# A DeltaNet layer in a streaming encoder: low parts of its weights on GpSimd, the state update in four row strips, the end of an inverse in whole-array products

## The chip, the cores and the metric

The kernel runs on one core of one Trainium2 chip. The metric is the device time of one execution in microseconds (us), lower is better. Engines are named as the profile names them: PE is TensorE (PEld its weight loads), DVE is VectorE, ACT is ScalarE, POOL is GpSimd and SP is SyncE, which issues most transfers.

## The reference

One inference step of a two-layer encoder for 384 tokens: 8 running streams of 16 tokens and one new stream of 256. Layer 0 mixes tokens by a convolution module, layer 1 by a gated DeltaNet; each layer has two SwiGLU sublayers and a cross-attention beside that. All is float32. The change concerns the DeltaNet of layer 1 (8 heads of 128):

```python
def gated_deltanet(h, conv_buf, S0, w_in, conv_w, a_log, dt_bias, norm_g, w_out):
    proj = h @ w_in
    ...
    qkv = jax.nn.silu(causal_depthwise_conv(hist, conv_w)).astype(F32)
    q, k, v = jnp.split(qkv, 3, axis=-1)
    q = l2_normalize(q.reshape(B, L, DN_HEADS, DN_HEAD_DIM)) * (DN_HEAD_DIM ** -0.5)
    ...
    o, S = chunk_gated_delta_rule(q, k, v, g, beta, S0.astype(F32))
    o = rms_norm(o, norm_g) * jax.nn.silu(gate.astype(F32).reshape(B, L, DN_HEADS, DN_HEAD_DIM))
    y = o.reshape(B, L, DN_WIDTH).astype(h.dtype) @ w_out
```

Within a block of tokens the rule solves a unit lower triangular system, and the state is carried on from block to block:

```python
    a_mat = jnp.where(strict, kk, 0.0) + jnp.eye(C, dtype=F32)
    sol = lax.linalg.triangular_solve(a_mat, rhs, left_side=True, lower=True, unit_diagonal=True)
    ...
        u = vc_i - jnp.einsum('bhck,bhkv->bhcv', kc_i, S)
        o = jnp.einsum('bhck,bhkv->bhcv', q_i, S) + jnp.einsum('bhij,bhjv->bhiv', qk_i, u)
        S = S * ge_i + jnp.einsum('bhck,bhcv->bhkv', kd_i, u)
```

## The kernel before, in words

**Tiles.** The 384 tokens are three tiles of 128: tile 0 the eight running streams (16 tokens each, so a strip of 32 partitions holds two streams), tiles 1 and 2 the new stream. Weights come in chunks of 128 x 1024 words.

**Weights in two parts.** TensorE multiplies a rounded type fast, so `get` (L276) loads a chunk, has ScalarE round it (high part, `whi`), and has VectorE subtract to get what the rounding lost (low part, `wlo`, L287, the operation itself in the helper `tt`, L197 in the profile). A projection (`proj` L725 with `gmm` L658) is then 24 products of 384 columns: for each of 8 slices of the depth high x high, high x low and low x high. Three raw and eight split chunks are on chip (L30, L31).

**Order of the work.** The program is recorded first. A main stream records projections one by one; generators (tasks) record what hangs on them, such as a head. `Scheduler.order` (L383) then sorts all recorded operations by a list schedule: each operation has a cost from a table in the helpers, the one with the longest way to the end goes first, and each engine gets a fixed order from it. Buffers and PSUM banks were given out while recording (eight banks, `_bank` L545, `gbank` L565), so a dependence through a bank is a dependence of the schedule too.

**The DeltaNet sublayer** (`deltanet`, L1249). The main stream projects gates first, then q, k, v of each head and the output gates z: 33 chunks (L1594 to L1610), then 8 chunks of the output projection (L1609). `short` (L1350) is the short convolution of one projected tile, with history copies on GpSimd (L215). `head` (L1369) does one head beside the main stream; a head's core waits for that of the head two before it (L1373), a q projection for the core of three before (L1598).

**The inverse** (`unit`, L1421), one for each of the three token tiles: blocks of up to 32 tokens are inverted by doubling, with masks that VectorE multiplies in (`apart`, L1433, two operands in SBUF) and products of 64 or 32 columns on TensorE. For tiles 1 and 2 the blocks of 32 are joined to 64 and these to 128; the last two products (L1464, L1467) use a quarter of the array:

```python
e = E.mm(g[64:128, 0:64], a[0:64, 64:128], x[0:64, 0:64], True, True)
e = E.act(y[64:128, 0:64], g[64:128, 0:64], dep=e, scale=-1.0)
yield max(e, e2)
e = E.mm(g[0:64, P:P + 64], y[64:128, 0:64], u[64:128, 64:128], True, True)
```

**The state's part of the running streams** is read by four products at once on tiles of 128 rows by 32 columns (`quad` L250, used at L1492).

**The state update** of the eight streams (L1541 to L1552), at the end of a head's core: in two rounds ScalarE makes four copies of `u`, each with the tokens of all but one stream set to zero (`K_BM`), TensorE multiplies the keys of all 128 tokens with the four copies (128 x 128 by 512 columns, float32, which TensorE does in two passes), and VectorE adds the 512 columns to the state. The state is then stored (L270).

Of the kernel before, what the change touches and what calls it, by code (L numbers as in the profile page):

```python
# [8 lines left out]
F32 = mybir.dt.float32  # L9
# [6 lines left out]
P = 128  # L16
D = 1024
KT = 8                  # feature tiles of d_model
NTOK = 384              # columns: 128 of the sample group (8 streams x 16), then 256 of the prompt
TT = 3                  # token tiles: sample, prompt 0, prompt 1  # L20
FF = 22                 # feature tiles of d_ff
NB = 8                  # sample streams
BL = 16                 # tokens of one
NH = 8                  # DeltaNet heads
XH = 4                  # cross-attention heads
# [4 lines left out]
W = 8                   # split weight chunks on chip  # L30
RAW = 3                 # raw chunks on chip  # L31
# order of the first transfers: memory (m), key and value chunks (c), rows (x), identity, gains
START = ["c0a", "m0a", "c0b", "m0b", "m1", "i", "x1", "g", "c1", "x2", "x0", "c2"]
TOLD = CW - BL          # taps that reach no token of the same step
OLD = 10                 # feature tile of the first sublayer from which these are worked on
CHB = 4000.0            # ns by which what belongs to a token tile goes before the same of the next
RUSH = 10000.0          # ns by which a sublayer's last projections go before the rest
NRUSH = 3               # feature tiles that this holds for
SLOTS = 4               # chunks of keys and values on chip at the start
FOUR = ["f01", "f10", "f11", "x0", "x1"]     # sublayers whose first 512 features are made token tile by token tile  # L40
# first projections of a sublayer that begin before the last token tile is there
SPLIT = {"f00": 0, "conv": 0, "x0": 1, "f01": 0, "f10": 0, "dn": 1, "x1": 2, "f11": 0}
# pieces of the memory's keys and values that a place in the program offers the tensor engine
KV = {"start": 3, "f00": 3, "conv": 20, "co": 3, "xo": 0, "f01": 1, "f10": 2, "dn": 6, "f11": 0}
HALF = 1400.0            # ns by which the first half of a row goes before the second
GROUPS = [(0, 1), (2, 3, 4, 5, 6, 7)]   # heads whose decays are made together
TAIL = 3                # down-projection chunks that go token tile by token tile
LANES = 8               # transfers under way on a queue
DMA_IN, DMA_OUT = 650.0, 950.0
HOP = 100.0             # ns from an engine to the next  # L50
BIG = 17300             # words of the shared region

# columns of the per-feature table
# [5 lines left out]
# constant matrices: causal blocks, block sums, decay masks, block-doubling masks  # L59
# [34 lines left out]
class Emitter:  # L94
    """Records the program in issue order. Tasks beside the main stream are advanced by running
    clocks of the engines, so that their matmuls fall where their operands are ready."""
# [153 lines left out]
    def quad(self, mms):  # L250
        """Products into four groups of 32 rows, which the tensor engine works on at once."""
        n = self._n(mms[0][2])
        cost = 2 * max(107.0, n / 1.2) + 85.0
        self.vt += cost
        t = self.nc.tensor

        def go():
            for out, lhsT, rhs, start, stop in mms:
                t.matmul(out, lhsT, rhs, start=start, stop=stop)  # L259
        self._add("P", cost, go, [x for m in mms for x in m[1:3]], [m[0] for m in mms])  # L260
        return self.vt + HOP

# [13 lines left out]
    def get(self, name, dest=None):  # L276
        """The two parts of a weight chunk: loaded and split as early as their room is free."""
        j = self.nchunk
        self.nchunk += 1
        raw = self.raw[j % RAW]  # L280
        hi, lo = dest if dest is not None else (self.hi[j % W], self.lo[j % W])
        assert dest is not None or j - W < 0 or self.held[j % W] is None, "a chunk is still in use"
        if dest is None:
            self.held[j % W] = j
        self.load(raw, self.wall[CHUNK[name]])
        self.act(hi, raw)
        self.tt(lo, raw, hi.bitcast(F32), ALU.subtract)  # L287
        return j, hi, lo
# [15 lines left out]
class Scheduler:  # L304
    """Orders the recorded program: a list schedule by the longest way to the end, on the engines'
    known costs, that keeps every dependence between the operations."""
# [8 lines left out]
    def cell(self, ap):  # L315
        """(what, bits): the tile and the columns in it that an operand covers."""
# [32 lines left out]
    def graph(self):  # L349
        ops = self.ops  # L350
        readers, writers = {}, {}
        for i, o in enumerate(ops):
# [3 lines left out]
            for what, bits in rs:  # L356
                if what is not None:
                    pred.update(j for b, j in writers.get(what, ()) if b & bits)
                    if what[0:2] == "ps":
                        # two engines don't read a bank at once  # L360
# [79 lines left out]
class Region:  # L440
    """First-fit allocation of the columns of one tile."""
# [5 lines left out]
    def take(self, n, keep=0, high=False):  # L447
# [13 lines left out]
        # of the places at an edge of a hole, the one whose columns were freed the longest ago  # L461
# [19 lines left out]
class Model:  # L481
# [42 lines left out]
    def alloc(self, n, keep=0):  # L524
        """(columns, handle) for the main stream."""
# [19 lines left out]
    def _bank(self):  # L545
# [3 lines left out]
        # the one that has been free for longest  # L549
# [38 lines left out]
    def rows(self, kind, i):  # L588
        """A row of gains on all partitions."""
# [4 lines left out]
    def rstd(self, s1, s2, dep):  # L594
        """(s1 + s2) ** -0.5."""
# [6 lines left out]
    def chain(self, t, y, yb, gpost, gpre, half=False, cross=False):  # L602
        """x += post(y); the next sublayer's normalized input, transposed and split."""
# [8 lines left out]
        if y is not None:  # L612
            ss, s0 = self.st(2), self.st(1)
            f = 4.0 if half else 1.0    # half of the norm: a root of four times the mean square
            for n in range(2):
                # the two banks, one to an engine at a time
# [15 lines left out]
        for n in range(2):  # L632
# [3 lines left out]
            # behind the row stands what its sum of squares is short of  # L636
# [21 lines left out]
    def gmm(self, out, hi, lo, c0=0, c1=NTOK, h=None, l=None):  # L658
        """out[feature, token] of a chunk [k, 8, 128 features] and the transposed activations."""
# [12 lines left out]
    def dmm(self, y, hi, lo, ah, al, first, last, halves=(0, 1)):  # L672
        """y[token, 1024] += activations [k, 128 tokens] times a chunk of rows."""
# [9 lines left out]
    def first_chunks(self, names, chains, split):  # L683
        """The first projections of a sublayer; some of them on two token tiles before the third is there."""
# [18 lines left out]
    def wide(self, o, w, t):  # L703
        """out[token, 512] of a token tile and four pieces of weights [k, 2, 512]."""
# [14 lines left out]
    def turn(self, a, o, e):  # L719
        """Four blocks of columns, transposed."""  # L720
# [4 lines left out]
    def proj(self, name):  # L725
        j, hi, lo = self.E.get(name)
# [5 lines left out]
    def gains(self, post, pre):  # L732
        """Rows of gains: of the norm behind a sublayer and of the next one's."""
# [98 lines left out]
    def tokenwise(self, acc, held, ops, ready, first, gpost, gpre, ghs, before=None, kv=0, late=False, half=False):  # L832
        """The last chunks of a product into the residual, token tile by token tile, each followed by
        its norms in the background."""
# [30 lines left out]
    def kv_open(self, slots=2, order=()):  # L865
        """Room for pieces of the memory's keys and values: the memory, some weight chunks, two results."""
# [14 lines left out]
    def early(self, what, order):  # L881
        """The first transfers of all go in a given order."""
        self.E.bonus = 1e9 - 1e6 * order.index(what) if what in order else 0.0

    def kv_part(self, out, name, what, order):
        """One of the first transfers in two halves, so that the products can begin with the first."""
# [16 lines left out]
    def kv(self, n):  # L903
        """Some pieces of the memory's keys and values. They wait for nothing else and go where the
        tensor engine would stand still."""
# [40 lines left out]
    def old_taps(self):  # L946
        """The taps that reach only tokens of earlier steps for all of a step's tokens."""
# [17 lines left out]
    def conv(self, chains, post, pre):  # L965
# [4 lines left out]
        HW = CW - TOLD + BL - 1     # tokens of a block and those before it that the later taps reach  # L970
# [27 lines left out]
        def taps():  # L998
            for c0 in range(0, KT, 2):
# [5 lines left out]
                for j in range(CW):  # L1005
                    for c in cs:
# [4 lines left out]
                        elif j < TOLD:  # L1011
                            # the prompt's tokens that have a token that far behind
# [236 lines left out]
    def deltanet(self, chains, post, pre):  # L1249
# [40 lines left out]
        def pre_task(o, b, e):  # L1290
            """Gates of all heads and the decays between all tokens."""
# [39 lines left out]
            for hs in GROUPS:  # L1331
# [12 lines left out]
                # one behind the other, so that the scalar engine changes its table once  # L1344
# [5 lines left out]
        def short(o, b, e, ti):  # L1350
            """Short convolution and SiLU of one feature tile; (columns, handle, ready)."""
# [17 lines left out]
        def head(h, q, k, v):  # L1369
# [51 lines left out]
            def unit(t):  # L1421
                """Decayed products of keys and queries, and the inverse's transpose by block doubling."""
# [6 lines left out]
                # blocks of up to 32 tokens lie one below the other in 32 columns: the transposes of the  # L1429
                # inverse so far and of what it makes of the matrix, which one product brings on together  # L1430
# [21 lines left out]
                if t:  # L1452
                    # pairs of blocks of 32 tokens, then the two of 64
# [10 lines left out]
                    e = E.mm(g[64:128, 0:64], a[0:64, 64:128], x[0:64, 0:64], True, True)  # L1464
                    e = E.act(y[64:128, 0:64], g[64:128, 0:64], dep=e, scale=-1.0)
                    yield max(e, e2)
                    e = E.mm(g[0:64, P:P + 64], y[64:128, 0:64], u[64:128, 64:128], True, True)  # L1467
# [21 lines left out]
            # sample: the state's part of the keys and queries, even and odd streams apart  # L1489
# [4 lines left out]
            # prompt, first chunk: no state yet  # L1494
# [46 lines left out]
            (UM, umh) = yield from room(512)  # L1541
# [248 lines left out]
```

## Time and profile before

| what | value |
|---|---|
| median of three runs | 1893.7 us (1892.61 to 1894.55) |
| span of the profiled execution | 1891.9 us |
| VectorE, ScalarE, GpSimd busy in it | 1025.5, 794.5, 168.8 us |
| mean granted TensorE clock | 0.998 |
| HBM | 146 GB/s over the span |

The profiled execution is one more run beside the three timed ones; its own time is known by its span, and 1.8 us lie between the span and the median of the runs. Rows of the profile give line, engine, operation, output<-inputs and shape, then the count, busy time, and the mean of one in ns. In a listing by time the first two numbers are start and length in us. TensorE's instructions are pipelined: their lengths overlap, and what one costs is read from the starts. A float32 product stands as two records, one for each pass.

### The profile page before, as it was taken

What the parts mean: (1) busy time and instruction counts of PE and PEld (TensorE: products, weight loads), DVE (VectorE), ACT (ScalarE), POOL (GpSimd) and SP (SyncE); (2) the same over time, 40 slices, a digit from 0 to 9 for tenths busy, and PEclk for the clock granted to TensorE, in tenths of its full rate; (3) what the DMA queues carried; (4) which work ended last, traced back from release to release, by engine and by line L of the source; (5) the groups of instructions that cost most, each with busy time, mean ns of one, the idle gap of its engine ahead of it and who ended that gap; (6) DMA issues with size and microseconds to landing.
All of it is one profiled execution on the core that took longest, in us unless ns stands there. A gap on an engine that the chain in (4) does not pass through costs nothing.

```text
span 1891.9 us, 27912 instructions
## 1 busy us (share of the span) xinstructions
PE 1870.6 (99%) x10863; PEld 1682.6 (89%) x10863; DVE 1025.5 (54%) x1940; ACT 794.5 (42%) x1589; POOL 168.8 (9%) x407
## 2 busy tenths in 40 slices
PE   8999999999999999999999999999999999999998
PEld 7999999999877899999899999989898767899997
DVE  6564436998653633334633344788886734533333
ACT  4333334312643533233433233787786533433332
POOL 1000002111100100000100000323321101000000
PEclk9999999999999999999999999999999999999999
DMA  8544434556685443434533343433324782444431
GB/s 300 179 136 125 134 112 121 128 147 216 219 312 210 156 129 128 134 123 130 163 122 117 120 134 101 128 97 99 123 90 124 236 311 101 134 134 134 122 123 45
DMA packets 88469, 278.83 MB, mean 147 GB/s; under 512 B 18001, under 2 KB 20561, under 8 KB 88337
## 3 DMA queue, kind: packets, MB, share of 16 engines
q1 hardware_dynamic: 86080, 271.42, 44.7%
q0 software_dynamic: 2256, 5.64, 0.9%
q8 instruction: 85, 1.39, 0.3%
q14 instruction: 48, 0.39, 0.1%
HBM read 265.09 MB, written 11.92 MB: 146 GB/s over the span
## 4 chain that ended last, share of the span: by engine, by line
PE 97%; ACT 1%; DMA 1%; DVE 0%; POOL 0%; issue 0%; SPq 0%; DVEq 0%; POOLq 0%; ACTq 0%
PE ps L247 91%; PE ps L266 3%; PE ps L259 2%; DMA raw<-in_w 0%; POOL stat L197 0%; ACT big L190 0%; DMA x<-in_x 0%; DVE big L210 0%; ACT whi L189 0%; SPq L270 0%; ACT big L189 0%; ACT hTl L190 0%; ACT L190 0%; DVE big L197 0%; DVE wlo L197 0%
## 5 line engine op out<-in xcount | busy, mean ns | idle before, releaser
L197 DVE TENSOR_TENSOR wlo<-raw,whi 128x1024 fp32r<-128x1024 f32 x361 | 438.1, 1221 | 570.7 <-ACT whi L189 542.7
L189 ACT CAST whi<-raw 128x1024 fp32r<-128x1024 f32 x361 | 374.5, 1050 | 640.3 <-PE ps L247 584.6
L247 PE MATMUL ps<-hTh,wlo 128*128 128x384 f32 x1680 | 498.3, 341 | 0.0
L247 PE MATMUL ps<-hTl,whi 128*128 128x384 f32 x1680 | 497.1, 342 | 0.0
L247 PE MATMUL ps<-hTh,whi 128*128 128x384 f32 (+1 forms) x1680 | 496.9, 342 | 0.0
L247 PEld LDWEIGHTS ps<-hTl,whi 128*128 128x128 f32 x1680 | 308.9, 188 | 8.0 <-issue 2.1
L247 PEld LDWEIGHTS ps<-hTh,whi 128*128 128x128 f32 x1680 | 308.8, 188 | 7.9 <-issue 1.2
L247 PE MATMUL ps<-big 128*128 128x128 f32 (+5 forms) x1944 | 308.0, 288 | 7.1 <-DMA big<-in_w 6.7
L247 PEld LDWEIGHTS ps<-hTh,wlo 128*128 128x128 f32 x1680 | 308.7, 188 | 6.5 <-issue 2.3
L247 PEld LDWEIGHTS ps<-big 128*128 128x128 f32 (+1 forms) x1944 | 269.6, 190 | 40.3 <-issue 20.8
L247 PE MATMUL ps<-whi,rbh 128*128 128x512 f32 x672 | 206.0, 396 | 0.4 <-ACT big L189 0.4
L247 PE MATMUL ps<-wlo,rbh 128*128 128x512 f32 x672 | 203.8, 395 | 0.0
L247 PE MATMUL ps<-whi,rbl 128*128 128x512 f32 x672 | 202.5, 393 | 0.0
L210 DVE SCALAR_TENSOR_TENSOR big<-big,cols 128x384 f32<-128x384 f32 (+13 forms) x424 | 189.5, 497 | 2.2 <-ACT big L190 0.3
L247 PEld LDWEIGHTS ps<-whi,rbl 128*128 128x128 f32 x672 | 125.7, 188 | 24.7 <-issue 0.4
L247 PEld LDWEIGHTS ps<-wlo,rbh 128*128 128x128 f32 x672 | 125.3, 188 | 24.6 <-issue 0.4
L247 PEld LDWEIGHTS ps<-whi,rbh 128*128 128x128 f32 x672 | 124.8, 188 | 21.1 <-ACT big L189 0.6
L197 DVE TENSOR_TENSOR big<-big,ps 128x64 f32<-128x64 f32 (+4 forms) x219 | 86.4, 405 | 39.8 <-PE ps L247 39.2
L266 PE MATMUL ps<-ident,big 128*128 128x128 f32 x479 | 89.5, 279 | 5.5 <-DVE big L210 5.4
L247 PE MATMUL ps<-whi,hTh 128*128 128x512 f32 x240 | 87.2, 399 | 0.7 <-ACT hTh L189 0.7
L189 ACT COPY big<-ps 32x32 f32<-32x32 f32 (+5 forms) x155 | 49.6, 324 | 90.2 <-PE ps L247 64.3
L247 PE MATMUL ps<-whi,hTl 128*128 128x512 f32 x240 | 86.3, 398 | 0.0
(82 smaller groups left out, 1350.7 us busy)
## 6 DMA issues: line engine op xcount, KB each, us to landing
raw<-in_w SPq DMA_DIRECT2D x362, 512.0 KB, 3.8
big<-in_w SPq DMA_DIRECT2D x37, 512.0 KB, 5.1
big<-in_ck SPq DMA_DIRECT2D x32, 512.0 KB, 6.5
big<-in_cv SPq DMA_DIRECT2D x32, 512.0 KB, 6.3
big<-in_npre SPq DMA_DIRECT2D x8, 512.0 KB, 7.5
out_pkv<-big POOLq DMA_DIRECT2D x32, 128.0 KB, 5.0
big<-in_npost SPq DMA_DIRECT2D x8, 512.0 KB, 7.3
big<-out_pkv SPq DMA_DIRECT2D x8, 512.0 KB, 5.1
```

The costliest lines, as they stand in the source:

```text
L189: return self._on("A", cost, dep, lambda: sc.copy(out, in_), [in_], w)
L197: return self._on(eng, cost, dep, lambda: e.tensor_tensor(out=out, in0=a, in1=b, op=op), [a, b], [out])
L210: lambda: v.scalar_tensor_tensor(out=out, in0=a, scalar=s, in1=b, op0=op0, op1=op1), [a, s, b], [out])
L247: self._add("P", cost, lambda: t.matmul(out, lhsT, rhs, start=start, stop=stop, **kw), [lhsT, rhs], [out])
L259: t.matmul(out, lhsT, rhs, start=start, stop=stop)
L266: self._add("P", 109.0, lambda: t.transpose(out, in_, ident), [in_, ident], [out])
```

## The change

Three edits, all inside the DeltaNet sublayer. Comments and docstrings were removed from the file as well.

1. `get` and `proj` take an engine. With "G" the low part is made by GpSimd, in two halves of 512 columns. The projections of the DeltaNet other than its first two chunks (31 chunks) and its 8 output chunks are made so; high parts stay on ScalarE, and all other sublayers stay as they were.
2. The last two products of the inverse take whole operands (128 rows, 128 columns of weights) and still 64 columns. The rows of the result that were not made before are not read, and the additional rows that are multiplied in hold zeros in the other operand.
3. The state update: ScalarE makes two masked copies of `u` (even streams, odd streams; `K_EO`), and four products follow, each on a strip of 32 tokens: its strip of the keys with 256 columns, into a bank of its own. VectorE adds four times 256 columns.

```diff
+    def strips(self, mms):
+        n = self._n(mms[0][2])
+        cost = 2 * max(107.0, n / 1.2) + 170.0
+        self.vt += cost
+        t = self.nc.tensor
+        def go():
+            for out, lhsT, rhs in mms:
+                t.matmul(out, lhsT, rhs, start=True, stop=True)
+        self._add("P", cost, go, [x for m in mms for x in m[1:3]], [m[0] for m in mms])
+        return self.vt + HOP
...
-    def get(self, name, dest=None):
+    def get(self, name, dest=None, eng="V"):
...
-        self.tt(lo, raw, hi.bitcast(F32), ALU.subtract)
+        if eng == "V":
+            self.tt(lo, raw, hi.bitcast(F32), ALU.subtract)
+        else:
+            for c in (slice(0, 512), slice(512, 1024)):
+                self.tt(lo[:, c], raw[:, c], hi[:, c].bitcast(F32), ALU.subtract, eng=eng)
...
-    def proj(self, name):
-        j, hi, lo = self.E.get(name)
+    def proj(self, name, eng="V"):
+        j, hi, lo = self.E.get(name, eng=eng)
...
-                    e = E.mm(g[64:128, 0:64], a[0:64, 64:128], x[0:64, 0:64], True, True)
+                    e = E.mm(g[:, 0:64], a, x[:, 0:64], True, True)
                     e = E.act(y[64:128, 0:64], g[64:128, 0:64], dep=e, scale=-1.0)
                     yield max(e, e2)
-                    e = E.mm(g[0:64, P:P + 64], y[64:128, 0:64], u[64:128, 64:128], True, True)
+                    e = E.mm(g[:, P:P + 64], y, u[:, 64:128], True, True)
...
-            (UM, umh) = yield from room(512)
-            bbm_ = cst[:, K_BM:K_BM + 8]
-            o, b = yield from self.gbank()
-            for j in range(2):
-                for n in range(4):
-                    em = E.act(tc_(UM, n), tc_(u, 0), dep=e4, scale=bbm_[:, 4 * j + n:4 * j + n + 1])
-                yield em
-                e4 = E.mm(o, tc_(kd, 0), UM, True, True)
-                c = slice(512 * j, 512 * j + 512)
-                e5 = E.tt(S[:, c], S[:, c], o, ALU.add, dep=max(e4, es2))
-                yield e5 - 800
+            (UM, umh) = yield from room(256)
+            for n in range(2):
+                em = E.act(tc_(UM, n), tc_(u, 0), dep=e4, scale=cst[:, K_EO + n:K_EO + n + 1])
+            (o0, b0), (o1, b1) = (yield from self.gbank()), (yield from self.gbank())
+            (o2, b2), (o3, b3) = (yield from self.gbank()), (yield from self.gbank())
+            yield em
+            os_ = (o0, o1, o2, o3)
+            r4 = [slice(32 * j, 32 * j + 32) for j in range(4)]
+            e4 = E.strips([(os_[j][:, 0:256], kd[r4[j], 0:P], UM[r4[j], :]) for j in range(4)])
+            for j in range(4):
+                c = slice(256 * j, 256 * j + 256)
+                e5 = E.tt(S[:, c], S[:, c], os_[j][:, 0:256], ALU.add, dep=max(e4, es2))
             E.load(self.O["sstate"][h], S)
-            self.bfree(b)
+            self.bfree(b0, b1, b2, b3)
...
-            o, b, e = fc[1] if n == 0 else self.proj((kind, h))
+            o, b, e = fc[1] if n == 0 else self.proj((kind, h), "G")
...
-        held = [E.get(("do", h)) for h in range(NH)]
+        held = [E.get(("do", h), eng="G") for h in range(NH)]
```

The costs in the helpers serve the ordering alone. For GpSimd the helper `tt` (L192) books 130 + 2.3 n ns for n columns, for VectorE 65 + 1.05 n; the new `strips` books 170 ns over the streaming of 256 columns in two passes, where `quad` books 85.

## The prediction

> **What bounds the kernel now.** The profile page first: span, engines, and the chain that ended last.
>
> ```profile
> span 1891.9 us, 27912 instructions
> PE 1870.6 (99%) x10863; PEld 1682.6 (89%) x10863; DVE 1025.5 (54%) x1940; ACT 794.5 (42%) x1589; POOL 168.8 (9%) x407
> PE 97%; ACT 1%; DMA 1%; DVE 0%; POOL 0%; issue 0%; SPq 0%; DVEq 0%; POOLq 0%; ACTq 0%
> ```
>
> TensorE (PE) is busy all the time and is 97% of the chain: what ends later or earlier is decided by the length of TensorE's own list, unless another engine makes it stand still. The profiled span, 1891.9 us, is 1.8 us under the median of the runs, 1893.7; I take that 1.8 as unchanged and subtract from the median.
>
> The change lies in the DeltaNet sublayer alone. Its products lie between about 1185 and 1485 us of the span, so the second view is the busy time by stage for that stretch (POOL is GpSimd), and for 30 us inside it in which VectorE (DVE) is fullest.
>
> ```profile
> core 0: us, PE busy (x) PEld busy (x) DVE busy (x) ACT busy (x) POOL busy (x), PEclk, DMA share, GB/s
> 1185.00:1485.00 300.00, 299.64 (x1997) 270.00 (x1995) 235.15 (x777) 225.20 (x667) 78.84 (x226) 1.00 0.35 113
> 1310.00:1340.00 30.00, 30.00 (x212) 26.28 (x211) 27.40 (x100) 23.41 (x79) 10.24 (x27) 1.00 0.36 113
> ```
>
> TensorE 299.64 of 300 at full clock; VectorE 235 (78%), ScalarE (ACT) 225 (75%), GpSimd 79 (26%). Even with VectorE at 27.4 of 30 (91%) TensorE did not stop. So here time off VectorE or ScalarE is worth nothing by itself, and time off TensorE's list is worth its full amount as long as the others follow.
>
> **What a product costs TensorE.** An instruction's own duration overlaps the next one's, so I read costs from starts, in the order of time. First a whole-array product of 64 columns among projections:
>
> ```profile
> 1417.18 0.33 PE L247 MATMUL ps<-hTl,whi 128*128 128x384 f32 x1
> 1417.35 0.33 PE L247 MATMUL ps<-hTh,wlo 128*128 128x384 f32 x1
> 1417.52 0.34 PE L247 MATMUL ps<-hTh,whi 128*128 128x384 f32 x1
> 1417.70 0.33 PE L247 MATMUL ps<-big 128*128 128x64 f32 x2
> 1417.84 0.42 PE L247 MATMUL ps<-hTl,whi 128*128 128x384 f32 x1
> 1418.10 0.34 PE L247 MATMUL ps<-hTh,wlo 128*128 128x384 f32 x1
> ```
>
> Projections follow each other every 0.175 us. From 1417.52 to 1418.10 are 0.58 us with two of them, so the float32 product between (two records) costs 0.58 - 0.35 = 0.23. Now the quarter-array product of the inverse:
>
> ```profile
> 1316.48 0.33 PE L247 MATMUL ps<-hTl,whi 128*128 128x384 f32 x1
> 1316.65 0.34 PE L247 MATMUL ps<-hTh,wlo 128*128 128x384 f32 x1
> 1316.92 0.74 PE L247 MATMUL ps<-big 64*64 64x64 f32 x4
> 1317.42 0.42 PE L247 MATMUL ps<-hTh,whi 128*128 128x384 f32 x1
> 1317.68 0.38 PE L247 MATMUL ps<-big 128*128 128x128 f32 x2
> ```
>
> The row of four holds the 64x64 product and a whole-array one behind it. 1316.65 to 1317.68 are 1.03; less two projections (0.35) and that whole-array product (0.23) the small one costs 0.45, twice the whole-array form: the projection ahead of it takes 0.27 instead of 0.175, and there is a toll behind it too. Third, the four products on 32-column tiles at once (L259), the form nearest to the new strips:
>
> ```profile
> 1250.55 0.44 PE L247 MATMUL ps<-hTh,wlo 128*128 128x384 f32 x1
> 1250.83 0.33 PE L247 MATMUL ps<-big 128*128 128x64 f32 x2
> 1250.96 0.42 PE L247 MATMUL ps<-hTh,whi 128*128 128x384 f32 x1
> 1251.32 0.64 PE L259 MATMUL ps<-big 128*32 128x256 f32 x8
> 1251.89 0.49 PE L247 MATMUL ps<-big 128*128 128x128 f32 x2
> 1252.13 0.42 PE L247 MATMUL ps<-hTl,whi 128*128 128x384 f32 x1
> 1252.39 0.27 PE L247 MATMUL ps<-big 128*128 128x128 f32 x1
> ```
>
> 1250.83 to 1252.39 are 1.56; less two projections and two whole-array products (0.81) the four cost 0.75 with both tolls. Fourth, the state update's product today:
>
> ```profile
> 1262.02 0.42 PE L247 MATMUL ps<-hTh,wlo 128*128 128x384 f32 x1
> 1262.27 0.34 PE L247 MATMUL ps<-hTh,whi 128*128 128x384 f32 x1
> 1262.45 1.02 PE L247 MATMUL ps<-big 128*128 128x512 f32 x2
> 1262.91 0.74 PE L247 MATMUL ps<-hTl,whi 128*128 128x384 f32 x1
> 1263.48 0.44 PE L247 MATMUL ps<-big 128*128 128x64 f32 x3
> ```
>
> 1262.27 to 1263.48 are 1.21; less two projections, 0.86 for one 128x512 float32 product.
>
> **The change part by part.** The counts first.
>
> ```profile
> L247 PE MATMUL ps<-big 128*128 128x512 f32 x32 | 16.4, 594 | 0.0
> L247 PE MATMUL ps<-big 64*64 64x64 f32 x64 | 10.2, 243 | 0.2 <-ACT big L189 0.2
> L197 DVE TENSOR_TENSOR wlo<-raw,whi 128x1024 fp32r<-128x1024 f32 x41 | 49.5, 1212 | 14.8 <-ACT whi L189 12.8 <-PE ps L247 2.0
> L210 DVE SCALAR_TENSOR_TENSOR big<-big,cols 128x384 f32<-128x384 f32 x72 | 43.4, 606 | 0.6 <-ACT big L190 0.3
> L197 DVE TENSOR_TENSOR big<-big 128x128 f32<-128x128 f32 x168 | 42.7, 277 | 0.5
> L197 DVE TENSOR_TENSOR big<-big,ps 128x512 f32<-128x512 f32 x14 | 9.4, 675 | 2.0 <-PE ps L247 2.0
> L190 ACT ACTIVATE big<-big 128x128 f32<-128x128 f32 x148 | 49.7, 383 | 8.8 <-DVE big L197 3.7 <-PE ps L247 2.9 <-PE ps L259 1.5
> ```
>
> *State update.* Two records make one float32 product, so the first row is 16 products, two to a head: 2 x 0.86 = 1.72 us a head go. Four strips of 32 tokens by 256 columns come. No trace shows strips of rows. If they overlap as the column tiles do they cost 0.75; if not at all, eight records of half a 512-column record (0.43, half of 0.86, so 0.215) are 1.72 plus the two tolls of about 0.1 each, 1.92. I take 0.86: the column tiles' price, and 0.1 because each strip loads weights of 128 columns, not 32, in both passes (the projection behind the shape change at 1250.55 takes 0.28 instead of 0.175, which is my measure of such a load with nothing to cover it). Saving 8 x 0.86 = 6.9 us, ends 7.8 and -1.6. The Trainium skill (TensorE: Matmul & The Clock Gate, Part 3, measured speedup against the span model) gives 3.07 times for four row strips of 512 columns; by it the eight records would take 0.56, with the tolls 0.76, and the saving would be 7.7.
>
> *Inverse.* 64 records are 32 products at 0.45, replaced one for one by whole-array products of 64 columns at 0.23: 0.22 each where one stands alone. Some stand beside another small-tile product and share a toll; I take 0.2, 6.4 us, ends 3.2 (every second toll shared) and 7.0.
>
> *ScalarE and VectorE in the state update.* Six of eight masked copies a head go: 48 x 0.383 = 18 us off ScalarE. VectorE's two adds of 512 columns become four of 256: between 277 ns (128) and 675 ns (512) lies 0.41, so 4 x 0.41 - 2 x 0.675 = 0.29 more a head, 2.3 us. From the masked copies to the last add a head's chain shortens from 2 x (4 x 0.383 + 0.86) + 0.675 = 5.5 us to 2 x 0.383 + 0.86 + 4 x 0.41 = 3.3. None of it is on TensorE's path today.
>
> *Low parts.* 31 projection and 8 output chunks: 39 x 1.212 = 47 us leave VectorE, 78 halves of 512 columns come to GpSimd. GpSimd's price for them is in no row; its nearest are copies:
>
> ```profile
> 1227.12 0.18 POOL L215 COPY big<-big 128x3 f32<-128x3 f32 x1
> 1233.20 0.21 POOL L215 COPY big<-big 128x32 f32<-128x32 f32 x1 [0.97 <-DVE big L210]
> 1289.54 1.14 POOL L215 COPY big<-big 128x24 f32<-128x24 f32 x1 [0.78 <-DVE big L210]
> 1289.39 1.22 DVE L197 TENSOR_TENSOR wlo<-raw,whi 128x1024 fp32r<-128x1024 f32 x1
> ```
>
> 0.03 us for 29 more columns is 1 ns a column: 0.7 us for 512 with one input, about 1.2 if the second input is read as slowly. I take 1.2, 94 us in all; ends 0.7 (55 us) and 2 (156 us). GpSimd would then be busy 173 of some 287 us. TensorE needs a low part only 24 products (4.2 us) at the soonest behind the previous chunk's, eight chunks have buffers, so two halves of 1.2 and a wait stay hidden; without that cover each would cost 2.4 - 1.2 = 1.2 us, 47 in all. Queued behind a half on GpSimd: the history copies that the short convolutions wait for, the some 15 small operations from which a head takes its scales, the sums and powers of the norms at both ends of the stage, and stores of keys and values. Each can come up to 1.2 us later.
>
> *The two engines in each other's way.* The last two rows: a copy that takes 0.21 took 1.14, from 1289.54 to 1290.68, 0.07 behind the end of the 1.22 us subtraction on VectorE that had begun before it. So a GpSimd read waits for a VectorE operation with two operands in SBUF. The Trainium skill (SBUF — State Buffer, SBUF: two separate sides) calls the shared port pair an exclusive lock for a whole instruction, in both directions; the trace agrees in this direction, 1.14 us against 0.21, and the other is not seen, as GpSimd's operations are short today. I price the other direction from rows: two SBUF operands have the 72 and the 168 of the list, 240 operations. With 94 us of halves in 287 a third of them meet one, with 0.6 us left: 240 x 0.33 x 0.6 = 47 us (ends 0 and 100). That is just what leaves: VectorE would stand at 235 - 47 + 2 + 47 = 237 of 287 us, 83%, below the 91% at which TensorE still ran. What I charge is latency: of a head's 21 two-operand steps in the inverse, some 8 in a row meet it, 8 x 0.2 = 1.6 us, with some 2 for GpSimd's queue, less the 2.2 by which the state update's chain shortens: 1.5 us at the last head, where no later projections cover it.
>
> *Whole operands, banks.* The whole-array forms read columns that were written earlier anyway: nothing. A state update holds four of eight PSUM banks for the strips and their adds instead of one: nothing as long as projections find a bank; otherwise see below.
>
> Sum: -6.9 - 6.4 + 1.5 = -11.8, 1881.9, say 1882.
>
> **The rivals.** *Banks (and the planner's new order).* With four banks held, TensorE's next projection waits for one. Each such wait is at most the four adds, 1.6 us; half of that for each of eight heads, and 6.4 us come back: 1888. For it: a head's unit holds its bank through the whole inverse. Against: today's wait for a bank isn't visible, PE 299.64 of 300.
>
> *Strips run one behind another.* Then the part that promises most does not do what it says: +1.6 in place of -6.9, 1890.4. Against: the L259 rows begin all eight records in 0.57 us.
>
> *VectorE becomes the bound (slower).* If a two-operand operation waits longer than I think, VectorE passes 91% of 287 us, 261. That needs 71 us of waits, 0.30 us for each of the 240, where I have 0.2. At 0.4 us, 96: 286 us of work, a stage of 286 / 0.91 = 314 instead of 300, and 1908. For it: every GpSimd copy caught behind a 1.2 us operation waited it out, and 78 such operations would now stand on the other side. Against: halves are spread, and a waiting VectorE operation gets in between two.
>
> **How the numbers follow.** Forecast 0.64 (1876 to 1886: strips 0.75 to 1.0, inverse 3.2 to 7.0, up to 3 us of waits), banks 0.18, strips in a row 0.07, VectorE 0.11. The range reaches from 1876 to 1893, which leaves out the VectorE case. 0.2%, 3.8 us, is about what a measurement of this kernel can tell from no change; faster means under 1889.9: 0.64, 0.14 of the banks' case and 0.03 of the strips in a row make 0.81; 0.08 lie within; 0.11 slower.
>
> **What would show it.** Right: eight strip groups whose records start within 0.05 us of each other, twice, and no 64x64 rows; the stage 11 to 13 us shorter; PE still over 99% in it; VectorE's rows for two SBUF operands longer or with idle time while a half runs; GpSimd's halves near 1.2 us. Wrong: strip records 0.2 us apart; TensorE idle with VectorE or GpSimd as releaser in the stage; halves over 2 us.

## The result, and the profile after

The change made the kernel slower: 1942.5 us (median of four runs, 1938.46 to 1943.55) against 1893.9 (four runs, the profiled one with them), a ratio of 1.0257 with a 95% interval of 1.0244 to 1.0269, 48.6 us. The page of the changed kernel, the lines that answer to those of before:

```profile
span 1936.7 us, 27984 instructions
PE 1886.9 (97%) x10895; PEld 1695.8 (88%) x10895; DVE 1036.5 (54%) x1917; ACT 781.2 (40%) x1539; POOL 261.6 (14%) x485
PE 88%; DVE 7%; ACT 2%; DMA 1%; issue 1%; POOL 1%; SPq 0%; DVEq 0%; POOLq 0%; ACTq 0%
```

TensorE's share of the chain fell from 97% to 88%, and VectorE, which had none, has 7%. The busy time by stage, for the DeltaNet (now some 350 us instead of 300), and for 14 us inside it:

```profile
core 0: us, PE busy (x) PEld busy (x) DVE busy (x) ACT busy (x) POOL busy (x), PEclk, DMA share, GB/s
1185.00:1535.00 350.00, 320.54 (x2055) 286.93 (x2054) 249.68 (x763) 213.84 (x625) 170.46 (x308) 0.95 0.32 105
1343.00:1357.00 14.00, 10.17 (x48) 7.60 (x48) 12.94 (x47) 4.09 (x18) 6.38 (x15) 0.53 0.36 117
```

TensorE is busy 320 of 350 us where it was busy 299.6 of 300, and its granted clock is 0.95, in the short stretch 0.53. VectorE has lost 47 us of subtractions and is still busy 250 us, but that is only 71% of the stage. Its groups in this stage, and GpSimd's halves (that last row is of the whole execution; 74 of the 78 lie in these 350 us):

```profile
L197 DVE TENSOR_TENSOR big<-big 128x128 f32<-128x128 f32 x168 | 64.7, 400 | 1.0
L210 DVE SCALAR_TENSOR_TENSOR big<-big,cols 128x384 f32<-128x384 f32 x72 | 60.4, 842 | 0.8
L215 DVE COPY big<-big 128x45 f32<-128x45 f32 x24 | 10.2, 426 | 7.5 <-ACT big L189 7.3
L197 DVE TENSOR_TENSOR big<-big,ps 128x256 f32<-128x256 f32 x32 | 12.3, 402 | 1.4 <-PE ps L272 1.4
L197 POOL TENSOR_TENSOR wlo<-raw,whi 128x512 fp32r<-128x512 f32 x78 | 104.3, 1347 | 313.0 <-ACT whi L189 312.3
```

The masks of the inverse take 400 ns instead of 277, the taps of the short convolution 842 instead of 606: those are the operations with two operands in SBUF. These are means: counted one by one, 42 of the 240 take over 0.1 us longer than usual, 0.87 us on average, and the others take what they took before. The adds that read PSUM are at 402, as interpolated (410). A listing by time shows one case from start to end:

```profile
1340.21 2.81 POOL L197 TENSOR_TENSOR wlo<-raw,whi 128x512 fp32r<-128x512 f32 x2
1340.24 1.66 DVE L210 SCALAR_TENSOR_TENSOR big<-big,cols 128x384 f32<-128x384 f32 x1
1341.83 1.35 DVE L197 TENSOR_TENSOR big<-big 128x128 f32<-128x128 f32 x1
1343.23 0.30 PEld L247 LDWEIGHTS ps<-big 128*128 128x128 f32 x2 [2.13 <-DVE big L197]
1343.23 0.43 PE L247 MATMUL ps<-big 128*128 128x64 f32 x2 [1.99 <-DVE big L197]
```

Two halves run on GpSimd from 1340.21 to 1343.02. A tap beside the first takes 1.66 us instead of 0.61; the mask behind it starts in the second half and ends at 1343.18, 0.16 behind it, 1.35 us instead of 0.28. The product of the inverse that needs the mask starts at 1343.23, and TensorE has stood still for 2 us. The clock is at half in the stretch that follows. The list of waits (us in total, times, longest), in the stage, sums such cases up:

```profile
PEld ps L247 <- DVE big L197: 26.3, 26, 2.6
PE ps L247 <- DVE big L197: 19.3, 20, 2.2
```

26 waits of TensorE's weight loads for this VectorE line, 26 us; the second row is in the main the same standstills, seen by the products. The kernel before has this in its stage (1185 to 1500 us):

```profile
PEld ps L247 <- DVE big L197: 0.6, 2, 0.4
```

### The profile page after: what moved, and what is told of

It reads as the page before. It is cut to its first block, busy times and chain, and to the rows that moved or that the text cites. A ratio compares the mean times of both kernels' runs of the same rounds, so it can differ in the third digit from the quotient of the medians.

```text
span 1936.7 us, 27984 instructions
## 1 busy us (share of the span) xinstructions
PE 1886.9 (97%) x10895; PEld 1695.8 (88%) x10895; DVE 1036.5 (54%) x1917; ACT 781.2 (40%) x1539; POOL 261.6 (14%) x485
## 4 chain that ended last, share of the span: by engine, by line
PE 88%; DVE 7%; ACT 2%; DMA 1%; issue 1%; POOL 1%; SPq 0%; DVEq 0%; POOLq 0%; ACTq 0%
PE ps L247 83%; DVE big L210 3%; PE ps L279 2%; PE ps L259 2%; DVE big L197 2%; DMA raw<-in_w 1%; ACT big L190 1%; POOL stat L197 1%; ACT whi L189 0%; DVE wlo L197 0%; DVE big L215 0%; DVE big L219 0%; DMA x<-in_x 0%; DVE x L210 0%; ACT L190 0%
## 5 line engine op out<-in xcount | busy, mean ns | idle before, releaser
L197 DVE TENSOR_TENSOR wlo<-raw,whi 128x1024 fp32r<-128x1024 f32 x322 | 392.0, 1226 | 556.0 <-ACT whi L189 530.2
L247 PE MATMUL ps<-hTh,whi 128*128 128x384 f32 x1680 | 498.1, 342 | 0.0
L247 PE MATMUL ps<-big 128*128 128x128 f32 (+3 forms) x1912 | 303.7, 290 | 27.6 <-DVE big L197 19.3
L247 PEld LDWEIGHTS ps<-big 128*128 128x128 f32 x1912 | 271.8, 196 | 63.0 <-DVE big L197 26.3
L210 DVE SCALAR_TENSOR_TENSOR big<-big,cols 128x384 f32<-128x384 f32 (+13 forms) x424 | 206.6, 537 | 2.4
L197 POOL TENSOR_TENSOR wlo<-raw,whi 128x512 fp32r<-128x512 f32 x78 | 104.3, 1347 | 313.0 <-ACT whi L189 312.3
L197 DVE TENSOR_TENSOR big<-big,ps 128x64 f32<-128x64 f32 (+5 forms) x235 | 88.0, 384 | 50.0 <-PE ps L247 48.1
L189 ACT CAST rbh<-big 128x384 fp32r<-128x384 f32 x84 | 43.1, 513 | 115.0 <-DVE big L197 95.2
```

The lines of the kernel that those rows point to most:

```text
L189: return self._on("A", cost, dep, lambda: sc.copy(out, in_), [in_], w)
L197: return self._on(eng, cost, dep, lambda: e.tensor_tensor(out=out, in0=a, in1=b, op=op), [a, b], [out])
L210: lambda: v.scalar_tensor_tensor(out=out, in0=a, scalar=s, in1=b, op0=op0, op1=op1), [a, s, b], [out])
L247: self._add("P", cost, lambda: t.matmul(out, lhsT, rhs, start=start, stop=stop, **kw), [lhsT, rhs], [out])
```

## The experiments

Theory A: VectorE's operations with two SBUF operands wait for GpSimd's halves, and TensorE for them. Rival B: the four PSUM banks, or the new order of the program, make TensorE wait. Each time stands against the kernel before as run with it.

**The parts alone.** `pe_only` keeps both TensorE edits and leaves the low parts on VectorE:

```diff
-            o, b, e = fc[1] if n == 0 else self.proj((kind, h), "G")
+            o, b, e = fc[1] if n == 0 else self.proj((kind, h))
-        held = [E.get(("do", h), eng="G") for h in range(NH)]
+        held = [E.get(("do", h)) for h in range(NH)]
```

> The two TensorE edits alone (row strips, whole-array products); all low parts on VectorE as before. Theory A, that VectorE's operations with two operands in SBUF wait for GpSimd's halves and TensorE for them: without the halves the saving of TensorE's list stands alone, 1878 to 1884 us. Theory B, that the four PSUM banks held by the strips and the order planned around them make TensorE wait: most of the loss stays, 1910 to 1945 us.

Measured 1892.0 us, ratio 0.9992 (0.9983 to 1.0002). The loss is gone, so it hangs on the halves; but the saving isn't there either.

`low_only` keeps the halves and undoes the state update and the inverse.

> GpSimd's halves alone; state update and inverse as before. Theory A: the whole loss and none of the saving, 1893.7 + 49 + 12, so 1940 to 1965 us. Theory B: 1890 to 1897 us, since VectorE is only relieved.

1934.8 us, ratio 1.0224 (1.0203 to 1.0245), +41: a little less than expected, and rival B's form is out for the large loss. With the TensorE edits on top it is 7 us worse, not 13 better.

`strips_only` undoes the inverse in `pe_only`, `whole_only` the state update.

> The row strips of the state update alone. Theory A: 8 x 0.86 us less, 1885 to 1889 us. Theory B: slower than before by 15 us or more, as the banks are held here too.

> The inverse's whole-array products alone. If the strips' four banks are what gave the saving back in the run of both TensorE edits: the 6.4 us are realised here, 1885 to 1889 us. If the stage's pace is set by the heads' chains on VectorE and ScalarE, so that a shorter list of TensorE only turns into waiting: 1891 to 1895 us.

`strips_only` 1894.3 us, 1.0008 (0.9998 to 1.0017): no gain, and no loss of 15 us either. `whole_only` 1890.4, 0.9986 (0.9978 to 0.9995): 2.6 us of 6.4, between the two forecasts. The strips themselves are as fast as forecast, as the order of time in `strips_only` shows:

```profile
1293.22 0.33 PE L247 MATMUL ps<-big 128*128 128x64 f32 x2
1293.36 0.42 PE L247 MATMUL ps<-hTh,wlo 128*128 128x384 f32 x1
1293.71 0.71 PE L272 MATMUL ps<-big 32*128 32x256 f32 x8
1294.36 0.66 PE L247 MATMUL ps<-big 128*128 128x64 f32 x4
```

1293.22 to 1294.36 are 1.14; less the whole-array product (0.23) and the projection (0.175) 0.74, and with the toll behind it (0.1) 0.84 against the 0.86 that I took. All eight records begin within 0.34 us, in two passes of four; so they do in six of the eight heads, and in the other two within 0.69 and 0.54.

**What of the halves costs.** `memset` keeps the changed kernel's order on every engine and takes away the reading:

```diff
-                self.tt(lo[:, c], raw[:, c], hi[:, c].bitcast(F32), ALU.subtract, eng=eng)
+                g = self.nc.gpsimd
+                lo_c = lo[:, c].bitcast(F32)
+
+                def go(o=lo_c):
+                    for _ in range(3):
+                        g.memset(o, 0.0)
+                self._on("G", 130 + 2.3 * 512, None, go, [raw[:, c], hi[:, c]], [lo[:, c]])
```

> The changed kernel with the same planned order on every engine, but each half on GpSimd is three fills with zeros, which read nothing in SBUF, instead of the subtraction. This leaves the low parts of 39 chunks out. Theory A, if only reading holds the port: VectorE's masks are back at 280 ns, its 384-column operations at 600 ns, TensorE's waits are gone, 1878 to 1890 us. Theory B, and any theory that blames the planned order or GpSimd's queue: as long as the changed kernel, 1935 to 1945 us.

1904.9 us, ratio 1.0064 (1.0049 to 1.0079): 37 of the 49 us are gone, which lies between the two forecasts. Its groups in the stage:

```profile
L310 POOL MEMSET wlo<- 128x512 f32 x234 | 122.2, 527 | 271.3 <-PE ps L247 262.1
L197 DVE TENSOR_TENSOR big<-big 128x128 f32<-128x128 f32 x168 | 45.2, 284 | 1.0
L210 DVE SCALAR_TENSOR_TENSOR big<-big,cols 128x384 f32<-128x384 f32 x72 | 43.6, 610 | 1.1 <-ACT big L190 0.3
L215 DVE COPY big<-big 128x45 f32<-128x45 f32 x24 | 6.0, 252 | 7.5 <-ACT big L189 7.3
```

GpSimd is busier than with the halves (122 against 104 us), yet masks and taps are back at 284 and 610. So it is not GpSimd's time that makes them wait, but what the fills leave out: the reading, and with it the subtraction. Against this run the three groups of the changed kernel are longer by 168 x 0.116 + 72 x 0.232 + 24 x 0.174 = 40 us, and the kernel loses 37. `memset1` fills each half once:

> As the run with fills in place of the subtractions, but one fill of about 0.53 us for each half instead of three; leaves the low parts of 39 chunks out. If the 11 us that stayed there come from small GpSimd operations queued behind the fills: 1890 to 1896 us. If they come from the order: 1901 to 1907 us.

1901.9 us, ratio 1.0048 (1.0035 to 1.0062): only 3 us less, so the queue on GpSimd isn't what stays.

> The changed kernel with low parts in four pieces of 256 columns on GpSimd. If a VectorE operation waits out the piece under way: the pieces last about 0.7 us, a wait is half as long, and of the 37 us that reading costs 12 to 20 come back, 1920 to 1932 us. If it is GpSimd's total reading time that counts, or the number of its operations: 1940 us or more.

`quarters` 1925.6 us, ratio 1.0175 (1.016 to 1.0191), 17 us less than the changed kernel. Its pieces take 0.81 us instead of 1.35; now 71 of the 240 operations wait, but 0.4 us each instead of 0.87: a wait gets shorter with the piece under way. `planned` adds 200 or 390 ns to the planner's cost of these operations:

> The changed kernel with the planner told of the waits: within the DeltaNet it books 0.2 us more for each VectorE operation with two operands in SBUF of up to 128 columns, 0.39 us more for longer ones. If the waits hurt because TensorE's order leaves them no room: 1905 to 1930 us. If they hurt because the heads' chains are longer whatever the order: 1935 to 1950 us.

1927.8 us, ratio 1.0191 (1.0178 to 1.0205): 15 us come back, though the same three groups are 42 us longer than with fills: 40 us of waits cost 37 us in the one order, 42 us cost 23 over `memset` in the other. Part of the loss is thus an order that gives the waits no room; most of it stays.

**What stays without reading.** `nolow_pe` leaves the subtraction out altogether:

> Both TensorE edits, and the low parts of the 39 DeltaNet chunks not made by any engine (old contents are multiplied; the low parts are left out). VectorE has 47 us less, none of it in a head's chain of steps. If VectorE's amount of work is what keeps TensorE's saving from showing: 1880 to 1886 us, as with the taps left out. If it is the length of the heads' chains, in which the taps are and the low parts are not: 1889 to 1895 us, and moving the low parts anywhere could have gained nothing.

1900.9 us, ratio 1.0042 (1.0028 to 1.0056). No theory had this: 47 us less on VectorE, and 9 us slower than `pe_only`, as slow as `memset1`. `noop_pe` leaves the same work out, but the planner still books it on VectorE:

```diff
+        elif eng is None:
+            self._on("V", 65 + 1.05 * D, None, lambda: None, [raw, hi], [lo])
```

> As nolow_pe (both TensorE edits, the low parts of 39 chunks left out, VectorE 47 us less), but planned as if VectorE still made them, so that every engine has the order of pe_only, without those subtractions. If the 9 us between pe_only and nolow_pe come from the order that the planner makes once it has the low parts off VectorE: 1888 to 1893 us. If less work on VectorE itself does harm, by a path not seen yet: 1898 to 1903 us.

1890.7 us, ratio 0.9988 (0.9978 to 0.9997). So the 9 us come from the order that the planner makes once it thinks the low parts off VectorE, and the 47 us themselves are worth some 1 us, less than these runs can tell from nothing. One stretch shows how an order can cost. In that of `nolow_pe` no projection starts between 1322.1 and 1333.0 us, only steps of the heads, and TensorE waits for them:

```profile
1325.26 0.43 PE L247 MATMUL ps<-big 128*128 128x64 f32 x2 [1.23 <-DVE big L197]
1326.41 0.55 PE L279 MATMUL ps<-ident,big 128*128 128x128 f32 x3 [0.71 <-ACT big L190]
1327.51 0.69 PE L279 MATMUL ps<-ident,big 128*128 128x128 f32 x2 [0.55 <-DVE big L197]
```

The clock falls to half at the end of these waits. The busy time from 1327 to 1338 us, first `nolow_pe`, then `noop_pe`:

```profile
1327.00:1338.00 11.00, 10.19 (x44) 8.99 (x45) 7.80 (x35) 4.13 (x17) 3.26 (x9) 0.53 0.23 91
```

```profile
1327.00:1338.00 11.00, 9.58 (x72) 7.91 (x72) 7.70 (x34) 8.93 (x39) 6.40 (x18) 1.00 0.55 156
```

At clock 0.53 TensorE begins 44 records there, at 1.00 it begins 72; in part these are other products, as the orders differ.

**Where TensorE's saving went.** Four banks, the heads' chains, or an order without room:

> The kernel before, but each head's state update holds three more PSUM banks without using them, from its first product to its last add. If banks are the cause: 5 to 12 us slower than before, 1899 to 1905 us. If not: within 3 us of before.

1894.4 us, ratio 1.0007 (0.9998 to 1.0016): holding the banks alone costs 1.4 us, if anything.

> Both TensorE edits, low parts on VectorE, and a planner that reckons 0.2 us more from ScalarE and VectorE to TensorE everywhere, so that TensorE's order leaves room for results that come late. If the saving is lost to an order without room: 1880 to 1887 us. If the work of the other engines is the limit: 1890 to 1895 us.

1892.8 us, ratio 1.0 (0.9991 to 1.0009): 0.2 us of room everywhere helps nothing.

`light_before` and `light_pe` drop the loop of three `E.stt` in `short`:

> The kernel before without three of the four taps of the short convolutions: 72 VectorE operations of 0.6 us, 43 us, are left out. TensorE's list alone sets its pace: within 3 us of before, 1890 to 1896 us. If the heads' chains already set it: 1885 us or less.

> Both TensorE edits, low parts on VectorE, and the same three taps left out. If the 13 us that TensorE's list lost were given back because VectorE's and ScalarE's work for the heads now sets the pace: the saving appears once VectorE has 43 us less, 1877 to 1885 us, some 10 under the kernel before with the same taps left out. If they were given back through banks or a worse order: 1889 to 1895 us.

1890.9 us, ratio 0.9987 (0.9978 to 0.9996), and 1884.9, ratio 0.9956 (0.9941 to 0.9971). Without the taps the same TensorE edits are worth 6 us instead of 1.4, where the forecast had some 10. `bare_pe` leaves out low parts as well, from the plan too, as `nolow_pe` does:

> Low parts and three taps left out together, both TensorE edits. By amount of work: 1878 to 1882 us, clearly below the run without the taps alone (1884.9). By the length of the chains: 1883 to 1887 us, the same as that run.

1884.1 us, ratio 0.9952 (0.9938 to 0.9966), the same as `light_pe`. Alone it doesn't rule out VectorE's amount of work, since taking the low parts out of the plan cost 9 us in `nolow_pe`; `noop_pe`, with the order kept, speaks against it. The taps lie in the heads' chains of steps; that it is the shorter chains which let the saving show is argued from this, as `light_pe` has an order of its own too.

`pairs` and `late_pe` change the strips of `pe_only`:

```diff
+            for j2 in (0, 2):
+                (o0, b0), (o1, b1) = (yield from self.gbank()), (yield from self.gbank())
+                os_ = (o0, o1)
+                e4 = E.strips([(os_[j][:, 0:256], kd[r4[j2 + j], 0:P], UM[r4[j2 + j], :]) for j in range(2)])
...
+                self.bfree(b0, b1)
+            yield e5 - 800
```

> Both TensorE edits, low parts on VectorE, the strips two at a time with two banks, and the head counted as done only behind the last add, as before. TensorE pays a second change of shape, about 0.65 us a head. If four banks at once cost more than that: 1884 to 1889 us. If not: 1890 to 1895 us.

> Both TensorE edits with all four strips at once, low parts on VectorE, and the head counted as done only behind the last add, as in pairs. If pairs won by its two banks: 1891 to 1894 us, as pe_only. If by the later end of the head: 1887 to 1890 us.

`pairs` 1889.8 us, ratio 0.9981 (0.9972 to 0.999), the lowest of those that do all of the work, though `whole_only` (0.9986) can't be told from it; `late_pe` (the last line of that diff alone) 1893.4, ratio 1.0003 (0.9994 to 1.0012). Two strips at a time are no slower than four although TensorE pays a second change of shape. With `banks_only` near nothing, I can't say whether the two banks or the order that came with them did it. How much of the lost saving is standstill shows in the 300 us from 1185, of which TensorE was busy 299.64 before; `pe_only`, `whole_only`, `pairs`:

```profile
1185.00:1485.00 300.00, 294.35 (x2018) 268.73 (x2016) 229.75 (x789) 207.15 (x616) 85.45 (x225) 1.00 0.35 114
1185.00:1485.00 300.00, 298.00 (x1996) 271.51 (x1995) 236.82 (x781) 227.05 (x673) 80.34 (x228) 1.00 0.36 116
1185.00:1485.00 300.00, 298.36 (x2021) 272.02 (x2020) 234.09 (x794) 202.94 (x614) 82.67 (x224) 0.99 0.36 117
```

In `pe_only` TensorE stands still for 5.65 us, 5.3 more than before; in `whole_only` for 2.0 and in `pairs` for 1.64.

## Why the prediction was wrong

The step that failed is the charge for VectorE and GpSimd standing in each other's way: "What I charge is latency ... 1.5 us at the last head, where no later projections cover it", and with it the point from which VectorE would decide, 91% of the stage.

- *The sum of the waits was nearly right, by luck.* 47 us was the estimate, 79 of the 240 operations with 0.6 us each. 42 of them waited, 0.87 us each, some 36 us; with the 45-column copies, which the estimate left out, the three groups took 40 us longer than with fills. Fewer and longer waits nearly cancel. GpSimd's half took 1.35 us, not 1.2. VectorE was busy 250 us where the sum said 237.
- *What they do to TensorE was wrong.* That VectorE at 91% had not stopped TensorE was no sign of a reserve: that order had been planned with this load in it. Each product of a head has a fixed place in TensorE's list; when its mask is 1 us late, the projections behind it, ready or not, wait too. And "later projections" are not always there to cover: between 1340.20 and 1355.05 us TensorE's list holds not one. The waits cost 37 us at 71% VectorE (changed kernel against `memset`). The rival named the right pair of engines but argued by the amount of work, and its 1908 us were too few.
- *The order itself* cost 9 us that were in no term (`nolow_pe` against `noop_pe`). Of the planner's new order the rival "banks" spoke only in its heading.
- *The clock* was in no term. Mean granted clock of the changed kernel and of the one before, of the span:

```profile
core 0: 1936.7 us, clock 0.989
```

```profile
core 0: 1891.9 us, clock 0.998
```

0.011 x 1936.7 = 21 us of clock were not granted, against 4 before: up to 17 of the 45 us between the two spans are TensorE at half speed after a wait, and part of these fall into further waits. For `nolow_pe` (0.994 of 1902.9) it is 11 against 4 for `pe_only` (0.998 of 1891.5), up to 7 of the 11 us between these two spans.
- *The savings.* Strips 0.84 against 0.86, right. That the subtractions leave VectorE for nothing was right (`noop_pe`). But "time off TensorE's list is worth its full amount as long as the others follow" hid the condition: they didn't follow. Of 13.3 us 1.4 showed, and by the interval it may be nothing. About 5 of the missing 12 are standstill (`pe_only`); that it is the heads' chains which take this back is supported by `light_pe`, where 6 us show. The rest isn't seen as idle time. In `whole_only`, of 6.4 us, 2.6 showed and TensorE stood still only 1.6 us more than before: the 0.45 and 0.23 were each read at one place, so the term may be too large, or small waits hide where lengths overlap. That stays open.
- *The range.* Its own terms (strips 0.75 to 1.0, inverse 3.2 to 7.0, 0 to 3 us of waits) give 1879 to 1888, not 1876 to 1886. The miss doesn't hang on it.

The whole 48.6 us, by differences of runs: both TensorE edits -1.4; an order with the low parts off VectorE +9 (`nolow_pe`); three fills on GpSimd instead of nothing +4, with the difference between the orders of `nolow_pe` and the changed kernel in it; reading instead of filling +37.

## What to carry to other kernels

When an engine is 99% busy in an order laid down in advance, read the slack of the chains that feed it, not the busy share of the engines in them: here 40 us of waits in such chains cost 37 us, and 42 us cost 23 where the planner knew of them. Before moving an elementwise operation to GpSimd, count VectorE's operations with two SBUF operands that will meet it; if the engine to be relieved doesn't set the pace (here 47 us off VectorE were worth some 1 us), nothing is to be won that could pay for it. Before writing such a move, time a kernel that leaves the work out and keeps the order (here `noop_pe`): it shows the most that the move can bring in that order.

## What the runs showed of the hardware

The Trainium skill (SBUF — State Buffer, SBUF: two separate sides) has VectorE's operations with two SBUF inputs blocked by GpSimd operations that read SBUF, and those by them. The trace agrees for the first direction: 400 against 284 ns for masks and 842 against 610 for taps between reading and filling, with the adds from PSUM unchanged at 402. A fill doesn't stop them, but it does stretch some of the 45-column copies of VectorE, 252 ns on average, against 178 in `pe_only`:

```profile
L215 DVE COPY big<-big 128x45 f32<-128x45 f32 x24 | 4.3, 178 | 0.3 <-ACT big L189 0.3
```

I had not expected that TensorE's clock halves so readily. In the changed kernel one wait of 2 us, from 1341.24 to 1343.23, stands between ten us in which TensorE is always busy (the row below) and the fall to 0.53 over the 14 us from 1343:

```profile
1331.00:1341.00 10.00, 10.00 (x70) 10.00 (x68) 5.61 (x21) 6.63 (x20) 3.11 (x11) 1.00 0.19 55
```

In `nolow_pe` it falls at the end of waits of 1.23, 0.71 and 0.55 us, close together. The Trainium skill (TensorE: Matmul & The Clock Gate, Part 1) ties the fall to an idle window of about 3.4 us; here neither the one wait nor the three together were that long.
